# Output projection in two halves with reordered weight splits, and a down product in groups of up to four tile pairs, in a hybrid decoder layer

## The chip, the core and the metric

The kernel runs on one core of a Trainium2 chip. Its engines are TensorE (PE, with its weight loads shown as PEld), VectorE (DVE), ScalarE (ACT), GpSimd (POOL) and SyncE (SP), whose queue issues the DMAs. The metric is the device time of one execution in microseconds; the median of three runs before the change is 1321.57 us (1320.02 to 1322.45). The profile is one execution of its own, of 1318.76 us.

## The reference

One layer of a decoder step over 1088 tokens (1024 of a prompt, 8 x 8 of decoding), with model width 1024 and all values in fp32:

```python
hn = rms_norm(x, norm_mix_gain)
proj = hn @ w_in
...                                   # retention (8 heads) -> o_r, windowed attention (8 heads) -> o_s
h = x + jnp.concatenate([o_r, o_s], axis=-1) @ w_out
hf = rms_norm(h, norm_ffn_gain)
h = h + jnp.square(jax.nn.relu(hf @ w_up)) @ w_down      # 1024 -> 4096 -> 1024
```

The retention state and the key and value caches are outputs too. The change touches the output projection (`w_out`), the second norm and the two products behind it.

## The kernel before

**Precision.** Each fp32 operand of a matmul is split into a high part (an ACT cast, L754) and a low part (a subtraction, L755), and a product is three matmuls (`mm3`, L179 to L181): high by high, low by high, high by low. `halve` does a split, `wsplit` does it for a 128 x 512 piece of weights, and its last argument names the engine of the low part. Split weights lie in two rings of four buffers, `wa` and `wb`; the raw ones come through `rawload` into rings of three.

**Tokens.** They are worked on as two sets `s` of 544, each as two halves `h` of `Q` = 272. A tile `m` is 128 of the 1024 output features.

**Order.** The program is traced by Python, and a scheduler that simulates the engines puts each engine's instructions in order: program order is the priority, each engine and DMA queue then runs its list in order and waits on semaphores. Buffers of a pool that is closed are given to a later pool tile by tile, when their last user is done.

**Retention and first token set.** For blocks t = 5, 6, 7 a retention block runs, then `out_proj(0, m)` for two tiles, then `mix_block`, which stores the gated retention output (`mr_hi_d`, `mr_lo_d`). `mix_load(s, half, pool)` reads the mix of a token set back: half "a" is attention, "r" is retention. `out_proj` loads one tile of weights (`wo_raw`, 1024 columns), splits its two halves, and for each h adds up eight k-blocks, the attention half first, in one accumulator in PSUM. Then it adds the input (`y`), stores the result (`y_d`) for the end, multiplies by the norm's gain (`f`) and adds squares to `acc`.

**Second token set.** `operands(0, m)` for all m forms the seven right operands B11, B21, B22, T1 to T4 of the up product (a seven-product scheme over 2 x 2 blocks) from `f`, split by ACT and DVE (`op_0h`, `op_0l`). Then `mix_load(1, "r")` and, for each m, `out_proj(1, m)` and `operands(1, m)`. `norm(s)` sums `acc` over the partitions with small matmuls, takes the power −0.5 on POOL, writes the result to `r_d` in DRAM in two DMAs and reads it back, spread over all partitions, as `rsf` in a third. For the second set it stands inside the first `up`.

**Up product.** `up(fp)` for fp = 0 to 15: `left` loads the weights of one of 16 column blocks (`wu`), forms combinations on POOL (`comb`, L932) and gives seven split pieces in the order `PROD`. Each meets the operands of both token sets in accumulators `psx`, `psy`, `psz`. DVE, ACT and POOL form the squared ReLU and its combinations `rt`, stored to `u_d`.

**Down product.** Eight groups g of two row blocks of `w_down` (`wd0a`, `wd0b`, ...). For each of seven products, in the order `DOWN`, the piece of each row block is split (low part on POOL), `ur` is loaded from `u_d` and split into `uh` and `ul`, and 4 x 2 accumulators `psd` take six matmuls each. After each product each accumulator is added to one of four sums `a` by DVE (L1045), or copied there by ACT (L1043) the first time; the accumulators go on through several products. `yt` (the stored `y_d`) is added at the end of groups 1 to 6, two or three tiles each.

The lines that set the order at the two hand-overs before:

```python
for m in range(8):
    operands(0, m)
mx0x.close()
operand_tiles(1)
mix_load(1, "r", ox.enter_context(pool("mxR", side="right")))
for m in range(8):
    out_proj(1, m, late)
    operands(1, m)
    if m == 1:
        norm(0)
```

Of the kernel before, what the change touches and what calls it, by code (L numbers as in the profile page):

```python
# [2 lines left out]

# [32 lines left out]
def hymba_layer(ctx: ExitStack, tc: tile.TileContext, a: dict, o: dict):  # L36
# [725 lines left out]
    def rawload(src, name, tag="raw", pl=None):  # L762
        raw = (pl or mw).tile([P, 1024], F32, tag=tag, name=name, bufs=3)
        nc.sync.dma_start(raw, src)
        return raw
# [11 lines left out]
    def out_proj(s, m, psum):  # L777
        raw = rawload(a["w_out"][m], f"wo{s}_{m}_raw")
        w = [wsplit(raw[:, i * 512 : i * 512 + 512], "wa", f"wo{s}_{m}_{i}", nc.vector) for i in range(2)]
        y = om.tile([P, 2, Q], F32, tag="y", name=f"y{s}_{m}", bufs=2)  # L780
        nc.sync.dma_start(y.rearrange("p h n -> p (h n)"), a["xY"][:, s, m, :])
        for h in range(2):
            ps = psum()
            for k in (4, 5, 6, 7, 0, 1, 2, 3):
                lh, ll = (w[k // 4][:, i, k % 4 * 128 : k % 4 * 128 + 128] for i in range(2))
                mh, ml = (mix[s, ("r" if k < 4 else "a") + x][:, k % 4, h, :] for x in "hl")
                mm3(ps, lh, ll, mh, ml, k == 4, k == 3)
            nc.vector.tensor_tensor(y[:, h, :], ps, y[:, h, :], ALU.add)
# [14 lines left out]

    def operands(s, m):
# [11 lines left out]
        else:  # L816
            put(B21, f[:, 0, :])
            put(B22, f[:, 1, :])
            b12, t1 = fs[s, kk][:, 1, :], fs[s, kk][:, 0, :]
            nc.gpsimd.tensor_tensor(t1, f[:, 1, :], t1, ALU.subtract)  # L820
            put(T2, t1)
            nc.gpsimd.tensor_tensor(f[:, 0, :], f[:, 0, :], t1, ALU.subtract)
            put(T4, f[:, 0, :])
            nc.gpsimd.tensor_tensor(f[:, 1, :], f[:, 1, :], b12, ALU.subtract)
            put(T3, f[:, 1, :])

    def norm(s):

        ps = psM.tile([P, 512], F32, tag="b", name=f"psr{s}")
        accf = acc[s].rearrange("p h n -> p (h n)")  # L830
        for i, r in enumerate((0, 128, 256, 384, 416)):
            col_sums(ps[:, i : i + 1], accf[:, r : r + 128], ones[:, 0:1])
        rf = (rst, nsinks)[s][:, 0:5]
        nc.vector.tensor_scalar(rf, ps[:, :5], 1.0 / 1024.0, EPS, ALU.mult, ALU.add)
        rsqrt_inplace(rf, 5)
        c0 = 2 * Q * s
        nc.sync.dma_start(r_d[c0 : c0 + 512].rearrange("(t p) -> p t", p=128), rf[:, :4])
# [30 lines left out]
    mx0 = mx0x.enter_context(pool("mx0", side="right"))  # L868
    mix_load(0, "a", mx0)
    mix_load(1, "a", mxA)  # L870
    mix_block(4, *held[4])
    mix_load(0, "r", mx0)
    early = lambda: psA.tile([P, 512], F32, tag="mm", name="pso")[:, :Q]
    for t in (5, 6, 7):
        mt = retention_block(t)
        for m in (2 * t - 10, 2 * t - 9):
            out_proj(0, m, early)
        mix_block(t, *mt)
    mix_block(8, *mt8)
    for m in (6, 7):  # L880
        out_proj(0, m, early)
# [24 lines left out]
    late = lambda: bank("pso")  # L906
    operand_tiles(0)
    for m in range(8):
        operands(0, m)
    mx0x.close()  # L910
    operand_tiles(1)
    mix_load(1, "r", ox.enter_context(pool("mxR", side="right")))
    for m in range(8):
        out_proj(1, m, late)
        operands(1, m)
        if m == 1:
            norm(0)
    ox.close()


    mid = ctx.enter_context(pool("u", side="right"))

    def left(order, src, name, lo_eng, raw_tag="raw", raw_pool=None, s_tag="S", s_pool=None, tags=("wa", "wb")):
# [6 lines left out]
        def comb(i, p_, q_, op):  # L930
            t_ = have[i] = (s_pool or mid).tile([P, 512], F32, tag=s_tag, name=f"{name}_s{i}", bufs=4)
# [11 lines left out]

    def up(fp):
        gen = left(PROD, a["w_up"][fp], f"wu{fp}", nc.vector)
# [229 lines left out]
```

## Time and profile before

| what | value |
|---|---|
| median of three runs | 1321.57 us |
| the profiled execution | 1318.76 us, span of its instructions 1317.0 us |
| PE busy | 1227.8 us (93%) |
| DVE busy | 842.5 us (64%) |
| POOL busy | 696.0 us (53%) |
| ACT busy | 504.5 us (38%) |
| DMA | 178.96 MB, 136 GB/s in the mean |

Times in the views are counted from the start of the span. By the lines of the kernel, the early projection begins at about 434, the last projection matmul starts at 594.5, the up product ends at 951 and the down product runs to the end. In a row of groups, `out<-in` are the tiles by their names in the program with numbers left out, then partitions x elements, `x` the count, busy time, mean time of one in ns, and the engine's idle time before them with what ended it. A wait is put down to the releaser that came last. PEclk is the granted share of the full clock of TensorE.

### The profile page before, as it was taken

How to read it: one execution, taken by the hardware profiler on the slowest of the kernel's cores; microseconds unless marked ns; L12 is line 12 of the kernel's file. 1: busy time of each engine (PE TensorE's matmuls, PEld its weight loads, DVE VectorE, ACT ScalarE, POOL GpSimd, SP SyncE). 2: the span in 40 equal slices, each digit the busy share in tenths (PEclk: the TensorE clock that was granted, in tenths of full speed). 3: DMA queues.
4: the chain of work that ended last, by engine and by line, in shares of the span. 5: the costliest groups of instructions: out<-in, count | busy, mean ns of one | idle time of the engine just before them, and what ended most of it. 6: DMA issues, size and time to landing. Idle time of an engine off the chain costs nothing.

```text
span 1317.0 us, 24166 instructions
## 1 busy us (share of the span) xinstructions
PE 1227.8 (93%) x9581; PEld 1161.9 (88%) x9581; DVE 842.5 (64%) x1549; ACT 504.5 (38%) x1027; POOL 696.0 (53%) x542
## 2 busy tenths in 40 slices
PE   7989999999998698595999999999959999999998
PEld 5979877778978698595999999999959999999998
DVE  8736645543136567486666666767455888888886
ACT  5333334354213324153444344444444333333331
POOL 8325232222324423225566666656685887789761
PEclk9989999999999899698999999999989999999999
DMA  6211223324405855562243424243544445545434
GB/s 222 66 55 56 76 78 96 114 79 127 124 35 183 283 185 166 117 186 71 108 152 124 171 105 183 93 183 112 202 159 142 154 157 178 167 153 157 142 103 170
DMA packets 112778, 178.96 MB, mean 136 GB/s; under 512 B 14048, under 2 KB 82592, under 8 KB 112408
## 3 DMA queue, kind: packets, MB, share of 16 engines
q1 hardware_dynamic: 112663, 177.41, 41.1%
q8 instruction: 75, 1.23, 0.4%
q14 instruction: 40, 0.32, 0.1%
HBM read 119.31 MB, written 58.07 MB: 135 GB/s over the span
## 4 chain that ended last, share of the span: by engine, by line
PE 77%; DMA 8%; DVE 7%; POOL 5%; issue 1%; ACT 1%; SPq 0%; DVEq 0%; ACTq 0%; POOLq 0%
PE psd L181 7%; PE psd L179 7%; PE psd L180 7%; PE psx L179 5%; PE psx L181 5%; PE psx L180 5%; PE psf L181 3%; PE psf L179 3%; PE psf L180 3%; PE psz L181 2%; PE psz L179 2%; PE psz L180 2%; PE pst L179 2%; PE pst L180 2%; PE pst L181 2%; PE po L421 2%
## 5 line engine op out<-in xcount | busy, mean ns | idle before, releaser
L1045 DVE TENSOR_TENSOR a<-a,psd 128x272 f32<-128x272 f32 x416 | 162.4, 429 | 43.8 <-PE psd L181 43.3
L755 DVE TENSOR_TENSOR ul<-ur,uh 128x1088 fp32r<-128x1088 f32 (+1 forms) x57 | 108.5, 1908 | 25.9 <-ACT uh L754 23.7
L367 POOL TENSOR_TENSOR sp<-sp,ssp 128x1024 f32<-128x1024 f32 (+1 forms) x16 | 28.6, 1787 | 110.0 <-DVE ssp L366 110.0
L179 PE MATMUL psx<-op_1h,wu_w 128*128 128x272 f32 x256 | 75.0, 293 | 7.1 <-ACT m L974 7.1
L755 DVE TENSOR_TENSOR wu_w<-wu_s,wu_w 128x512 fp32r<-128x512 f32 x64 | 69.9, 1093 | 15.9 <-ACT wu_w L754 14.7
L179 PE MATMUL psx<-op_0h,wu_w 128*128 128x272 f32 x256 | 74.9, 292 | 0.0
L181 PE MATMUL psx<-op_1l,wu_w 128*128 128x272 f32 x256 | 74.7, 292 | 0.0
L181 PE MATMUL psx<-op_0l,wu_w 128*128 128x272 f32 x256 | 74.5, 291 | 0.0
L180 PE MATMUL psx<-op_1h,wu_w 128*128 128x272 f32 x256 | 74.3, 290 | 0.0
L180 PE MATMUL psx<-op_0h,wu_w 128*128 128x272 f32 x256 | 74.1, 289 | 0.0
L961 DVE SCALAR_TENSOR_TENSOR m<-m,rsf 128x272 f32<-128x272 f32 x96 | 61.8, 644 | 11.9 <-DMA rsf<-r_d 9.2
L754 ACT CAST uh<-ur 128x1088 fp32r<-128x1088 f32 (+1 forms) x57 | 61.8, 1087 | 9.0 <-PE psd L180 9.0
L181 PE MATMUL psf<-hnl,wqk_hi 128*128 128x384 f32 (+1 forms) x192 | 65.0, 339 | 0.0
L995 POOL TENSOR_TENSOR rt<-rt 128x272 f32<-128x272 f32 x64 | 64.3, 1014 | 1.2
L179 PE MATMUL psf<-hnh,wqk_hi 128*128 128x384 f32 (+1 forms) x192 | 64.9, 338 | 0.0
L180 PE MATMUL psf<-hnh,wqk_lo 128*128 128x384 f32 (+1 forms) x192 | 64.8, 338 | 0.0
L995 POOL TENSOR_TENSOR rt<-r,rt 128x272 f32<-128x272 f32 x32 | 31.7, 992 | 62.0 <-ACT r L962 62.0
L755 DVE TENSOR_TENSOR wu_w<-wu_r,wu_w 128x512 fp32r<-128x512 f32 x48 | 41.6, 868 | 27.5 <-ACT wu_w L754 27.5
L179 PEld LDWEIGHTS psx<-op_1h,wu_w 128*128 128x128 f32 x256 | 48.8, 191 | 7.3 <-ACT m L974 7.3
L956 DVE TENSOR_TENSOR m<-m,psz 128x272 f32<-128x272 f32 x64 | 28.0, 437 | 41.5 <-ACT m L974 26.6
L754 ACT CAST wu_w<-wu_s 128x512 fp32r<-128x512 f32 x64 | 39.8, 622 | 37.4 <-PE psy L181 30.5
L403 DVE SCALAR_TENSOR_TENSOR sp<-dtab,nsl,scp 128x256 f32<-128x256 f32 (+1 forms) x64 | 28.5, 459 | 37.4 <-PE scp L402 37.0
(511 smaller groups left out, 4902.8 us busy)
## 6 DMA issues: line engine op xcount, KB each, us to landing
u_d<-rt SPq DMA_DIRECT2D x32, 952.0 KB, 5.7
ur<-u_d SPq DMA_DIRECT2D x56, 544.0 KB, 4.0
wu_r<-in_w_up SPq DMA_DIRECT2D x32, 512.0 KB, 4.2
wo_raw<-in_w_out SPq DMA_DIRECT2D x16, 512.0 KB, 4.1
y<-in_xY SPq DMA_DIRECT2D x16, 272.0 KB, 3.0
y_d<-y SPq DMA_DIRECT2D x16, 272.0 KB, 2.4
yt<-y_d SPq DMA_DIRECT2D x16, 272.0 KB, 3.6
out_yT<-a SPq DMA_DIRECT2D x16, 272.0 KB, 2.2
```

The costliest lines, as they stand in the source:

```text
L179: nc.tensor.matmul(ps, lh, rh, start=first, stop=False, skip_group_check=more)
L180: nc.tensor.matmul(ps, ll, rh, start=False, stop=False, skip_group_check=more)
L181: nc.tensor.matmul(ps, lh, rl, start=False, stop=last, skip_group_check=more)
L367: nc.gpsimd.tensor_tensor(s, s, ss.unsqueeze(2).broadcast_to([P, 4, n]), ALU.mult)
L403: nc.vector.scalar_tensor_tensor(s[:, g, :], dtab[:, 256 - n :], nsl[:, c, kv, g : g + 1], pg, ALU.mult, ALU.add)
L421: nc.tensor.matmul(po[p_, :], vs[:, c - 1 + h, p_], pts[kv][:, h, :], start=h == halves[0], stop=h == 1)
L754: nc.scalar.copy(hi, src)
L755: lo_eng.tensor_tensor(lo, src, hi.bitcast(F32), ALU.subtract)
L956: nc.vector.tensor_tensor(t_, t_, bank_, ALU.add)
L961: nc.vector.scalar_tensor_tensor(t_, src, 0.0, rsf[:, s, h, :], ALU.max, ALU.mult)
L995: sub = lambda o_, p_, q_: nc.gpsimd.tensor_tensor(o_, p_, q_, ALU.subtract)
L1045: nc.vector.tensor_tensor(to, to, ps, ALU.add)
```

## The change

The projection's weights are loaded for two tiles at a time and one half of the rows at a time (`wo_pair`). For the first token set the splits of a tile pair are drawn one tile ahead (`out_early`), and the second set's attention mix is loaded after block 6 and not at the start. For the second set, the attention halves of tiles 0 to 3 are accumulated first, in eight open accumulators; then four of the eight operand tiles of set 0 are formed, the retention mix is loaded, and the rest follows in pairs of tiles, with the other four operand tiles between them. The first two pieces of up weights are split before the last two residuals. `norm` spreads its result by matmuls with a broadcast operand and copies, and not by way of DRAM. In `operands` B22 comes last.

The down product runs in five groups of 2, 4, 4, 4 and 2 row blocks: each accumulator takes up to twelve matmuls before it is added to the sums. The weights' low parts are formed by DVE. The ring `rawb` has nine buffers instead of three, `Sb` ten instead of four. The `yt` adds stand at the end of groups 1 and 2, eight each. The up stage's own tiles get a pool that is closed with it.

```diff
-    def out_proj(s, m, psum):
-        raw = rawload(a["w_out"][m], f"wo{s}_{m}_raw")
-        w = [wsplit(raw[:, i * 512 : i * 512 + 512], "wa", f"wo{s}_{m}_{i}", nc.vector) for i in range(2)]
+    def wo_pair(s, m, half):
+        raw = mw.tile([P, 1024], F32, tag="raw", name=f"wo{half}{s}_{m}_raw", bufs=3)
+        c0 = 512 * (half == "a")
+        nc.sync.dma_start(
+            raw.rearrange("p (m n) -> p m n", m=2), a["w_out"][m : m + 2, :, c0 : c0 + 512].rearrange("m p n -> p m n")
+        )
+        for i in range(2):
+            yield wsplit(raw[:, i * 512 : i * 512 + 512], "wa", f"wo{half}{s}_{m + i}", nc.vector)
+
+    def out_half(s, half, ps, h, w, first, last):
+        for k in range(4):
+            lh, ll = (w[:, i, k * 128 : k * 128 + 128] for i in range(2))
+            mh, ml = (mix[s, half + x][:, k, h, :] for x in "hl")
+            mm3(ps, lh, ll, mh, ml, first and k == 0, last and k == 3)
+
+    def residual(s, m, pss):
         y = om.tile([P, 2, Q], F32, tag="y", name=f"y{s}_{m}", bufs=2)
...
+    def out_parts(s, ms, half, psum, pss):
+        for m in ms:
+            if m % 2 == 0:
+                gen = wo_pair(s, m, half)
+            w = next(gen)
+            for h in range(2):
+                if half == "a":
+                    pss[m, h] = psum()
+                out_half(s, half, pss[m, h], h, w, half == "a", half == "r")
...
     def norm(s):
-        rsqrt_inplace(rf, 5)
-        c0 = 2 * Q * s
-        nc.sync.dma_start(r_d[c0 : c0 + 512].rearrange("(t p) -> p t", p=128), rf[:, :4])
-        nc.sync.dma_start(r_d[c0 + 512 : c0 + 544].rearrange("(p t) -> p t", t=1), rf[96:128, 4:5])
-        nc.sync.dma_start(
-            rsf[:, s, :, :].rearrange("p h n -> p (h n)"), r_d[c0 : c0 + 544].unsqueeze(0).broadcast_to([P, 544])
-        )
+        rsqrt_inplace(rf, 6)
+        for h in range(2):
+            pb = psM.tile([P, 512], F32, tag="b", name=f"psn{s}{h}")
+            for i, (c0, n) in enumerate(((0, 128), (128, 128), (256, 16))):
+                nc.tensor.matmul(
+                    pb[:, c0 : c0 + n], rf[:, 3 * h + i : 3 * h + i + 1].broadcast_to([P, 128]), ident[:, 128 - n :],
+                    start=True, stop=True,
+                )
+            nc.scalar.copy(rsf[:, s, h, :], pb[:, :Q])
...
+    def out_early(m):
+        if m % 2 == 0:
+            gens["a"], gens["r"] = (wo_pair(0, m, x) for x in "ar")
+            ahead.extend(next(gens[x]) for x in "ar")
+        wa_, wr_ = ahead
+        ahead.clear()
+        if m % 2 == 0:
+            ahead.extend(next(gens[x]) for x in "ar")
+        pss = [early() for h in range(2)]
+        for h in range(2):
+            out_half(0, "a", pss[h], h, wa_, True, False)
+            out_half(0, "r", pss[h], h, wr_, False, True)
+        residual(0, m, pss)
...
     mix_load(0, "a", mx0)
-    mix_load(1, "a", mxA)
...
+        if t == 6:
+            mix_load(1, "a", mxA)
         mix_block(t, *mt)
...
+    pss = {}
+    out_parts(1, range(4), "a", late, pss)
+    for m in (2, 6, 3, 7):
+        operands(0, m)
+    mx0x.close()
+    operand_tiles(1)
+    mix_load(1, "r", ox.enter_context(pool("mxR", side="right")))
+    rest = [0, 4, 1, 5]
+    for ms in ((0, 1), (2, 3), (4, 5), (6, 7)):
+        if ms[0] > 3:
+            out_parts(1, ms, "a", late, pss)
+        out_parts(1, ms, "r", late, pss)
+        if ms == (6, 7):
+            gen0 = left(PROD, a["w_up"][0], "wu0", nc.vector, tags=("wa", "wa", "wb", "wb"))
+            ready = [next(gen0), next(gen0)]
+        for m in ms:
+            residual(1, m, [pss[m, h] for h in range(2)])
+            if rest:
+                operands(0, rest.pop(0))
+            operands(1, m)
+        if ms == (2, 3):
+            norm(0)
...
-    for g in range(8):
-        gens = [
-            left(DOWN, a["w_down"][2 * g + 1], f"wd{g}b", nc.gpsimd, "rawb", dn, "Sb", dn, ("wb",)),
-            left(DOWN, a["w_down"][2 * g], f"wd{g}a", nc.gpsimd, tags=("wa",)),
-        ]
+    for g, (f0, nf) in enumerate(((0, 2), (2, 4), (6, 4), (10, 4), (14, 2))):
+        gens = []
+        for f in range(nf):
+            own = ("rawb", dn, "Sb", dn) if f else ("raw", mw, "S", mid)
+            gens.append(left(DOWN, a["w_down"][f0 + f], f"wd{f0 + f}", nc.vector, *own, tags=("wb" if f % 2 else "wa",)))
...
-                    for f in range(2):
+                    for f in range(nf):
...
-        for n in range(16):
-            if n * 6 // 16 + 1 == g:
+        if g in (1, 2):
+            for n in range(8 * g - 8, 8 * g):
```

More of the change, by code (lines that the diff above doesn't have):

```diff
@@ L2 @@
 from contextlib import ExitStack
+from itertools import chain
 import numpy as np
@@ L782, in out_proj @@
         for h in range(2):
[L783 to L788, printed above, removed]
+            nc.vector.tensor_tensor(y[:, h, :], pss[h], y[:, h, :], ALU.add)
         kk, k2 = m % 4, m // 4
@@ L942, in left @@
             yield wsplit(have[i], tags[n % len(tags)], f"{name}_w{i}", lo_eng)
+    late = lambda: bank("pso")
+    operand_tiles(0)
+    pss = {}
[20 more added lines that the diff above has]
+            norm(0)
+    ox.close()
+    mid = ctx.enter_context(pool("w", side="right"))
+    ux = ExitStack()
+    um = ux.enter_context(pool("u", side="right"))
     def up(fp):
[L945 removed]
+        gen = chain(ready, gen0) if fp == 0 else left(
+            PROD, a["w_up"][fp], f"wu{fp}", nc.vector, tags=("wa", "wa", "wb", "wb"))
         x, y, z = ([bank(f"ps{n}{s}") for s in range(2)] for n in "xyz")
         home = {1: (x, True), 2: (y, True), 6: (x, False), 5: (z, True), 7: (x, False), 4: (x, False), 3: (z, False)}
[L948 removed]
+        rt = [um.tile([P, 7, Q], F32, tag="rt", name=f"rt{fp}_{s}", bufs=2) for s in range(2)]
         held, wait = {}, []
         def tq(n, s):
[L952 removed]
+            return um.tile([P, Q], F32, tag="tq", name=f"{n}{fp}_{s}", bufs=10)
         def add(n, s, bank_):
@@ L1004, in hymba_layer @@
     opx.close()
+    ux.close()
     dn = ctx.enter_context(pool("dn", side="left"))
```

64 lines of the change are left out of this document (23 added, 41 removed).

## The prediction

> **What bounds the kernel now.** I read the page first, for the share of each engine.
>
> ```profile
> span 1317.0 us, 24166 instructions
> PE 1227.8 (93%) x9581; PEld 1161.9 (88%) x9581; DVE 842.5 (64%) x1549; ACT 504.5 (38%) x1027; POOL 696.0 (53%) x542
> ```
>
> The matrix engine PE is busy for 93%, but an average over stages hides where it stops. So the second view is the table of windows, one row for each stage that the change touches: columns are busy us and instructions of PE, weight loads, DVE, ACT, POOL, then granted clock, DMA share and GB/s.
>
> ```profile
> 415.00:507.00 92.00, 76.72 (x748) 71.87 (x747) 59.71 (x135) 28.22 (x48) 30.23 (x22) 0.91 0.72 234
> 507.00:595.00 88.00, 67.53 (x520) 66.60 (x519) 58.46 (x106) 34.19 (x78) 30.66 (x32) 0.84 0.57 152
> 595.00:629.00 34.00, 19.97 (x164) 19.30 (x163) 21.23 (x29) 12.41 (x29) 18.58 (x15) 0.77 0.26 63
> 629.00:951.00 322.00, 322.00 (x2551) 321.81 (x2551) 207.09 (x316) 139.17 (x316) 202.93 (x182) 1.00 0.38 142
> 951.00:992.00 41.00, 23.51 (x157) 22.63 (x157) 20.62 (x8) 17.50 (x40) 32.78 (x28) 0.83 0.54 186
> 992.00:1317.00 325.00, 318.56 (x2549) 317.90 (x2547) 262.59 (x484) 112.63 (x162) 232.01 (x149) 1.00 0.48 151
> ```
>
> From 629 to 951 (the up product) PE never stops: 322/2551 = 0.126 us per matmul. At that pace the other stages need: 507–595, 520 x 0.126 = 65.5 of 88 us (22.5 lost); 595–629, 20.7 of 34 (13.3 lost); 951–992, 19.8 of 41 (21.2 lost); 992–1317, 321.2 of 325 (3.8 lost). In 415–507, where small matmuls of the retention are mixed in, PE is idle for 92 − 76.7 = 15.3 us. So about 76 us can be had at all, nearly all of it in the three hand-overs: retention to output projection, projection to up, up to down. The clock falls to 0.77–0.84 there, so the loss is more than the idle time. The waits of PE name the places (total us, times, longest):
>
> ```profile
> PE pso L179 <- DMA mixrh<-mr_hi_d: 11.9, 2, 10.3
> PE psd L181 <- DVE ul L755: 11.3, 1, 11.3
> PE pso L180 <- DVE wo L755: 10.7, 3, 6.1
> PE psx L179 <- ACT m L974: 7.1, 1, 7.1
> PE psy L179 <- ACT wu_w L754: 4.3, 1, 4.3
> PE pso L179 <- ACT wo L754: 3.9, 2, 3.7
> PE psd L179 <- DVE a L1045: 2.6, 2, 1.6
> PE psy L180 <- DVE wu_w L755: 2.6, 1, 2.6
> ```
>
> **The change, part by part.** Matmuls of the projection and the down product, weight loads and bytes stay the same in number; what moves is order, owner and latency.
>
> *A, start of the projection (415–507).* Loading the second token half's attention mix moves from the head of the queue to behind block 6.
>
> ```profile
> 420.00:430.00 10.00, 6.90 (x76) 6.10 (x76) 7.65 (x19) 2.37 (x4) 4.50 (x4) 0.83 1.06 396
> 417.84 0.62 SPq L773
> 418.51 0.85 SPq L773
> 419.41 14.14 DMA wo_raw<-in_w_out
> ```
>
> The first two rows of the chain are the issues of this pair (128 x 4 x 544 fp32 each, 2.2 MB); the first projection weights queue behind them and land 14.14 us later, with the DMA engines full at 396 GB/s. 2.2 MB at 396 GB/s is 5.6 us. The first `wo` splits, and the q/k loads of the next retention block behind them, come 5.6 us sooner; PE's 3.7 us wait for `wo` goes, and the retention chain is late next. The pair lands later, at a DMA share below this one. Each early pair of tiles now needs two raw loads, but each holds two tiles' halves: the same 512 KB per tile. Bounds: −2 (the moved pair delays block 7's loads) to +12; I take a gain of 5.
>
> *B, projection of the second token half and its operands (507–604).*
>
> ```profile
> 507.00:604.00 97.00, 71.29 (x582) 69.91 (x580) 66.66 (x118) 40.34 (x93) 36.58 (x38) 0.85 0.52 141
> L755 DVE TENSOR_TENSOR op_1l<-f,op_1h 128x272 fp32r<-128x272 f32 x28 | 17.2, 649 | 1.5 <-ACT op_1h L754 1.5
> L755 DVE TENSOR_TENSOR op_0l<-f,op_0h 128x272 fp32r<-128x272 f32 x28 | 17.0, 657 | 1.2 <-DMA y<-in_xY 1.2
> 537.36 0.33 SPq L764 DMA_DIRECT2D wo_raw<-in_w_out  x1
> 538.38 0.38 SPq L837 DMA_DIRECT2D r_d<-rst  x1
> 538.86 13.68 DMA mixrh<-mr_hi_d
> ```
>
> Before, all 28 splits `op_0l` stand ahead of the next weights on DVE, so PE waits for `wo` (10.7 in all); then `mixrh` is issued at 538.86, behind a weight load and the norm's `r_d` on SP, lands 13.68 us later, and PE waits 10.3. After, four tiles' attention halves run first: 4 x 2 x 12 matmuls = 96 x 0.126 = 12.1 us of PE work that needs neither, and it covers both waits. `norm(0)` and its DMAs come behind the load. The other half of the operands is dealt out between the later tiles. What is late next is DVE: its work is the same 66.7 us, and without gaps it would end at 507 + 66.7 = 573.7 instead of 604. Eight accumulators stay open until DVE's residual adds close them, so PE will wait for DVE at times. I take DVE filled to 81% (as the down product fills it: 262.6/325), 82 us, so the operands end at 589: a gain of 15. Bounds: 0 (same gaps) to 30 (none).
>
> *C, into the up product (595–629).* The chain there:
>
> ```profile
> 607.47 1.56 POOL nsinks L133
> 609.47 9.47 DMA r_d<-nsinks
> 618.99 4.84 DMA rsf<-r_d
> L626 PE MATMUL pkr<-c_ident,kt 128*128 128x128 f32 x24 | 4.3, 299 | 0.0
> L974 ACT COPY m<-psx 128x272 f32<-128x272 f32 x94 | 35.4, 382 | 39.6 <-PE psx L181 39.5
> ```
>
> The norm's way through DRAM takes from 609.03 to 623.83, 14.8 us; it becomes six matmuls (nearest row, a transpose of one block, 0.299) and two copies of 0.382: 1.8 + 0.8, with hand-overs about 3 us. It is 12 us shorter, and three issues leave SP. New is that PE's queue holds matmuls that wait for POOL's 1.56 us power, with the up product behind them: 0 to 4 us for each norm, by the order. Two up weights are split before the last residual, so the `wu_w` waits (4.3 + 2.6) go. `B22` is put last, and is needed last. The stage's loss is 13.3, of which 10 go; bounds 2 to 13.3.
>
> *D, into the down product (951–992).*
>
> ```profile
> 971.32 15.34 DVE L755 TENSOR_TENSOR ul<-ur,uh 128x1088 fp32r<-128x1088 f32 x2 [11.81 <-ACT uh L754]
> L755 DVE TENSOR_TENSOR ul<-ur,uh x57: 812/1566/14142, 955.7 to 1302.3; 128x1088 fp32r<-128x1088 f32 x55, 128x544 fp32r<-128x544 f32 x2
> 972.00 1.29 POOL L932 TENSOR_TENSOR wd1a_s<-wd1a_s,wd1a_r 128x512 f32<-128x512 f32 x1
> ...
> 983.06 1.25 POOL L932 TENSOR_TENSOR wd1b_s<-wd1b_r,wd1b_r 128x512 f32<-128x512 f32 x1
> u_d<-rt SPq DMA_DIRECT2D x32, 952.0 KB, 5.7
> ```
>
> One `ul` takes 14.14 us where the median is 1.57: POOL runs without a gap beside it, its last instruction in the row ends at 984.3, and `ul` ends at 985.5. PE waits 11.3 of it. The weights' low parts leave POOL, so its ready queue shrinks: of the ten in this row, four are splits (their `w` tiles). But POOL keeps the 16 `rt` subtractions and now may work ahead on ten `Sb` tiles: up to 10 x 1.27 = 13 us in a row, so a shorter stall can come back. Also the new pool (nine raw, ten `Sb` buffers) is larger than the operands' space and reaches into that of the up stage, so an accumulator may wait for the last `u_d` store, whose landing takes 5.7 us: 0 to 5.7. Bounds −4 to +18; I take 12.
>
> *E, inside the down product (992–1317).*
>
> ```profile
> L1045 DVE TENSOR_TENSOR a<-a,psd 128x272 f32<-128x272 f32 x416 | 162.4, 429 | 43.8 <-PE psd L181 43.3
> L755 DVE TENSOR_TENSOR ul<-ur,uh 128x1088 fp32r<-128x1088 f32 (+1 forms) x57 | 108.5, 1908 | 25.9 <-ACT uh L754 23.7
> L1053 DVE TENSOR_TENSOR a<-a,yt 128x544 f32<-128x544 f32 x16 | 17.3, 1084 | 8.2 <-DMA yt<-y_d 8.0
> L755 DVE TENSOR_TENSOR wu_w<-wu_s,wu_w x58: 679/1180/1267, 629.8 to 934.3; 128x512 fp32r<-128x512 f32 x58
> ```
>
> Five groups instead of eight: 5 x 56 evictions, 32 of them copies, so 248 DVE adds instead of 416 (−168 x 0.429 = −72 us). Against it 112 splits come from POOL. Cheapest: 112 x 0.679 = 76; dearest, 112 x 1.267 = 142 (the up stage's largest). POOL was busy 63% in the up stage (202.9/322) and has only 64 combinations left here, 64 x 1.27 = 81 us, 24% of the stage; scaling the excess with POOL's share gives about 0.85 a split (95 us), and `ul` falls from its mean of 1.9 to about 1.5 (56 x 1.5 = 84). DVE: 248 x 0.429 + 95 + 84 + 17 = 302 us, beside PE's (157 + 2549) x 0.126 = 341. PE stays the bound; the split's price is hidden by it. The eight `yt` adds in a row in two groups can hold DVE for a load each, but a four-pair group gives DVE 7 x 12 x 0.126 = 10.6 us before a bank is needed again. Gain 0; bounds +3.8 and the rival below.
>
> **The sum.** 5 + 15 + 10 + 12 + 0 = 42. The profiled execution took 1318.76 us (span 1317.0): 1276.8. The median shown, 1321.57, is 2.8 higher, so I forecast 1280.
>
> **Rivals.**
> 1. *Slower: DVE becomes the bound of the down product.* It decides if a split's mean goes over (341 − 106 − 84 − 17)/112 = 1.2 us, near the dearest row (1.267), or less if DVE, in order, keeps its 44 us of waiting for PE: then 302 + 44 = 346 already touches 341. At the dear end, 349 + 44 = 393, 52 over 341; against gains of 30 elsewhere that is 1321.6 + 52 − 30 = 1344; half of it gives 1318. For it: DVE was 81% busy here (262.6/325). Against: POOL, which makes splits dear, loses most of its work. 0.12.
> 2. *The projection's gain is eaten by DVE's queue.* Both kinds of operands and the residual adds compete, PE stalls on open accumulators; B gives 0–3 and C 5: 1321.6 − 5 − 2 − 5 − 12 = 1298. For it: DVE is 69% busy there (66.7/97). 0.18.
> 3. *The port stall returns at the start of down* with the new work-ahead: D is 0, 1292. 0.17.
> 4. *More than forecast*: A to D come to their upper bounds, 12 + 30 + 13.3 + 18 = 73, 1248. For it: PE alone would need no more. Against: DVE's order would have to be without gaps. 0.07.
> 5. *The stall at the start of down goes wholly.* If DVE gets its port after one POOL instruction (1.3 us), the long `ul` came from something that does not return, and D gains 18: 1274. Against: the long `ul` itself, which outlasted ten POOL instructions. 0.08. The Trainium skill states such a rule, "SBUF — State Buffer", section "SBUF: two separate sides": DVE with two SBUF inputs and GpSimd take a shared port pair as a lock for one whole instruction, and the other blocks. By that rule the sum would be 1274, by the trace's 14.14 us it is 1280, and the measurement decides. The same rule speaks against the change in E, since it turns 112 splits into instructions of the kind that block and are blocked; the rows above price that.
> The forecast itself, 1265–1290, has 0.38.
>
> **How the numbers follow.** Leaving out the dear half of rival 1 and the far end of rival 4, the range is 1254–1314. A change of 0.2% (2.6 us) is about what can be told. Slower needs rival 1 near its dear end: 0.08; within 0.2%: its middle, 0.04; faster: 0.88.
>
> **What would show it.** A: the first `wo_raw` lands in under 10 us and PE's `wo` wait goes. B: no PE wait for `mixrh` over 2 us, operands done before 590 less A's gain. C: no `r_d` DMA of the norm; under 4 us between the power and the `rsf` copies; PE at full clock within 10 us of the last projection matmul. D: no `ul` over 4 us, first 40 us of down at over 280 matmuls. E: DVE near 300 us, POOL near 100, PE waits on L1045's successor below 4. Wrong if PE in the down product waits on DVE for more than 10 us, or if a new single wait over 10 us stands in a hand-over.

## The result, and the profile after

The changed kernel takes 1312.86 us in the median of five runs (1309.19 to 1316.79), the kernel before 1322.14 beside it (1320.02 to 1323.84): ratio 0.9935, 95% interval 0.9907 to 0.9963. That is 9.3 us faster where 42 were forecast. The profiled execution took 1311.57 us. Its page and its windows, with the columns of before:

```profile
span 1309.3 us, 24034 instructions
PE 1233.3 (94%) x9621; PEld 1167.0 (89%) x9621; DVE 832.6 (64%) x1492; ACT 496.5 (38%) x1030; POOL 529.6 (40%) x430
```

```profile
415.00:507.00 92.00, 79.23 (x756) 73.89 (x756) 60.25 (x136) 28.82 (x49) 31.52 (x23) 0.91 0.71 230
507.00:595.00 88.00, 70.30 (x564) 69.65 (x563) 61.82 (x110) 36.76 (x85) 31.61 (x33) 0.88 0.47 155
595.00:629.00 34.00, 28.43 (x245) 27.81 (x244) 25.87 (x37) 15.48 (x36) 23.51 (x19) 0.85 0.19 63
938.00:990.00 52.00, 32.44 (x228) 31.72 (x229) 28.77 (x27) 25.02 (x54) 35.41 (x26) 0.80 0.67 233
990.00:1309.00 319.00, 315.87 (x2511) 315.65 (x2509) 251.12 (x413) 106.23 (x152) 65.36 (x42) 1.00 0.44 143
```

In 507 to 595 PE is busy only 2.8 us more than before; from 595 to 629 it gains 8.5. In 938 to 990, the way into the down product, 19.6 us are still empty. The waits of PE name why:

```profile
PE psd L180 <- ACT uh L755: 19.4, 2, 17.2
PE pso L180 <- DMA mixrh<-mr_hi_d: 13.2, 1, 13.2
PE rsr L180 <- ACT qkb L608: 9.1, 5, 3.3
PE psn L860 <- POOL rst L134: 2.9, 1, 2.9
```

Two single waits of over 10 us stand in the hand-overs again: the one for `mixrh` is longer than before (10.3), and one of 17.2 us for `uh` has taken the place of the 11.3 for `ul`. The queue of SP shows both places, first at the mix, then at the end of the up product:

```profile
535.17 0.34 SPq L796 DMA_DIRECT2D y<-in_xY  x1
537.77 0.37 SPq L782 DMA_DIRECT2D wor_raw<-in_w_out  x1
538.19 0.57 SPq L774 DMA_DIRECT2D mixrh<-mr_hi_d  x1
...
944.41 0.33 SPq L765 DMA_DIRECT2D wd_r<-in_w_down  x1
946.67 4.42 SPq L1056 DMA_DIRECT2D u_d<-rt  x2
951.14 1.38 SPq L765 DMA_DIRECT2D wd_r<-in_w_down  x2
952.62 0.83 SPq L1080 DMA_DIRECT2D ur<-u_d  x1
```

`mixrh` goes out at 538.19 (before 538.86), and `ur` at 952.62, behind the last two stores `u_d`. Marks from the traces (start of a matmul, us), for the kernels that the text needs:

| kernel | last projection matmul | matmul 130 of up | last of up | first of down | matmul 200 of down | end |
|---|---|---|---|---|---|---|
| before | 594.5 | 630.3 | 952.7 | 955.7 | 999.3 | 1317.0 |
| changed | 590.9 | 618.5 | 944.2 | 961.7 | 992.6 | 1309.3 |
| norm_alone | 587.6 | 615.1 | 938.0 | 941.0 | 985.4 | 1302.5 |
| f67_in_rsf | 580.8 | 608.4 | 933.5 | 950.8 | 982.3 | 1299.0 |
| two_pools | 591.7 | 619.3 | 948.3 | 952.2 | 989.7 | 1306.4 |
| old_down | 587.9 | 617.1 | 939.5 | 943.0 | 973.4 | 1292.0 |
| proj_f67_dve_all | 577.5 | 607.0 | 935.0 | 938.4 | 968.4 | 1286.2 |

### The profile page after: what moved, and what is told of

Same layout as the page of the kernel before. It is cut to its first block, busy times and chain, and to the rows that moved or that the text cites. A ratio compares the mean times of both kernels' runs of the same rounds, so it can differ in the third digit from the quotient of the medians.

```text
span 1309.3 us, 24034 instructions
## 1 busy us (share of the span) xinstructions
PE 1233.3 (94%) x9621; PEld 1167.0 (89%) x9621; DVE 832.6 (64%) x1492; ACT 496.5 (38%) x1030; POOL 529.6 (40%) x430
## 4 chain that ended last, share of the span: by engine, by line
PE 67%; DMA 10%; DVE 8%; POOL 7%; issue 4%; ACT 3%; SPq 0%; ACTq 0%; POOLq 0%; DVEq 0%
PE psd L181 9%; PE psd L180 9%; PE psd L182 9%; POOL rt L1051 6%; DMA u_d<-rt 6%; PE psf L182 3%; PE psf L180 3%; PE psf L181 3%; PE pst L180 2%; PE pst L181 2%; PE pst L182 2%; PE po L422 2%; PE psx L181 2%; PE psx L182 2%; PE psx L180 2%
## 5 line engine op out<-in xcount | busy, mean ns | idle before, releaser
L180 PE MATMUL psd<-uh,wd_w 128*128 128x272 f32 x896 | 259.8, 290 | 19.4 <-ACT uh L755 19.4
L181 PE MATMUL psd<-uh,wd_w 128*128 128x272 f32 x896 | 260.8, 291 | 0.0
L182 PE MATMUL psd<-ul,wd_w 128*128 128x272 f32 x896 | 256.0, 289 | 0.0
L180 PEld LDWEIGHTS psd<-uh,wd_w 128*128 128x128 f32 x896 | 170.9, 191 | 19.8 <-ACT uh L755 19.8
L181 PEld LDWEIGHTS psd<-uh,wd_w 128*128 128x128 f32 x896 | 170.3, 190 | 0.0
L182 PEld LDWEIGHTS psd<-ul,wd_w 128*128 128x128 f32 x896 | 168.1, 189 | 0.3 <-DVE ul L756 0.3
L1099 DVE TENSOR_TENSOR a<-a,psd 128x272 f32<-128x272 f32 x248 | 102.4, 432 | 47.4 <-PE psd L182 47.4
L756 DVE TENSOR_TENSOR wu_w<-wu_s,wu_w 128x512 fp32r<-128x512 f32 x64 | 62.6, 981 | 95.9 <-ACT wu_w L755 95.8
L756 DVE TENSOR_TENSOR ul<-ur,uh 128x1088 fp32r<-128x1088 f32 x56 | 86.9, 1580 | 2.9 <-ACT uh L755 2.9
L755 ACT CAST wd_w<-wd_s 128x512 fp32r<-128x512 f32 x64 | 37.3, 618 | 111.1 <-PE psd L182 77.6
L1018 ACT ACTIVATE rt<-m 128x272 f32<-128x272 f32 x64 | 26.0, 427 | 111.1 <-DMA u_d<-rt 104.1
L956 POOL TENSOR_TENSOR wd_s<-wd_r,wd_s 128x512 f32<-128x512 f32 x16 | 24.6, 1538 | 104.5 <-DVE wd_w L756 103.3
```

The source lines that it names most:

```text
L180: nc.tensor.matmul(ps, lh, rh, start=first, stop=False, skip_group_check=more)
L181: nc.tensor.matmul(ps, ll, rh, start=False, stop=False, skip_group_check=more)
L182: nc.tensor.matmul(ps, lh, rl, start=False, stop=last, skip_group_check=more)
L755: nc.scalar.copy(hi, src)
L756: lo_eng.tensor_tensor(lo, src, hi.bitcast(F32), ALU.subtract)
L956: nc.gpsimd.tensor_tensor(t_, p_, q_, op)
```

## The experiments

All ratios are to the kernel before, run beside each, with their 95% intervals; that kernel's medians lay between 1320.4 and 1321.4.

### What holds the load of the retention mix back

`f67_low` only moves the addresses of `f6` and `f7`, so that the new mix covers exactly the old one:

```diff
+    f67 = {m: mx0.tile([P, 2, Q], F32, tag=f"f{m}", name=f"f0_{m}") for m in (6, 7)}
     mix_load(0, "a", mx0)
...
-            f = mx0.tile([P, 2, Q], F32, tag=f"f{m}", name=f"f{s}_{m}")
+            f = f67[m]
```

> The change as it is, with one thing different: the two scaled tiles f6 and f7 of the first token set lie below the mix tiles in their pool, so that the second set's retention mix no longer overlaps them. Queue theory: the load of that mix stays where it is in SP's list, behind the input tile y_1 and the weights wor_4, because the list holds it back until the last reader of the whole closed pool is placed. It is issued at 538 us (within 1), PE waits 13 us for it, the time stays within 2 us of the changed kernel's (0.992 to 0.995 of the kernel before). Address theory: the overlap was what it waited for; it is issued at 519 to 525, PE's wait falls below 4 and the time falls by 8 to 10 us (ratio 0.985 to 0.988).

Measured: 1313.56 us, 0.9948 (0.9929 to 0.9967); the load stays where it was, and PE's wait is 13.5 us.

```profile
538.56 0.57 SPq L774 DMA_DIRECT2D mixrh<-mr_hi_d  x1
```

`f67_in_rsf` takes both tiles out of the pool:

```diff
-            f = mx0.tile([P, 2, Q], F32, tag=f"f{m}", name=f"f{s}_{m}")
+            f = rsf[:, m - 6]
```

> The change, with f6 and f7 of the first token set in the still unused norm tile (rsf) and not in the pool of the first set's mix. Queue theory: that pool's last reader is now PE's last retention matmul of the first set at 518, so the load of the second set's retention mix stands ahead of y_0, woa_4 and wor_4 in SP's list, is issued at 515 to 521 (538 before), lands by 532, and PE's single wait of 13.2 us falls below 4. The last projection matmul starts 7 to 11 us sooner (591 to about 582) and the time falls by 6 to 10 us (ratio to the kernel before 0.986 to 0.989). Rival, DVE paces the stage: the load is sooner but DVE's operands and weight splits end where they did; another wait of PE (for a weight split or a bank) takes the place, the last projection matmul stays within 3 us of 591, the time within 3 us.

Measured: 1299.98 us, 0.9848 (0.9826 to 0.9869). Its SP queue and its window:

```profile
517.96 0.57 SPq L774 DMA_DIRECT2D mixrh<-mr_hi_d  x1
```

```profile
507.00:595.00 88.00, 75.39 (x638) 74.41 (x638) 68.60 (x121) 40.18 (x93) 38.91 (x39) 0.91 0.50 157
```

The load goes out 20 us sooner, the wait for it is gone, and 638 matmuls run in the window instead of 564. Since the address alone changes nothing, it is the place in SP's list: here and in the next pair of runs, a load into the space of a closed pool stands behind the last readers of that pool, here the splits of `f6` and `f7`, and so behind `y`, `woa` and `wor` loads that wait for DVE. The section on the kernel before says that a closed pool's buffers are given on tile by tile; for the place in the queue's list it is the whole pool that counts. The same edit with the old projection and the norm by matmuls:

> The kernel before with two of the edits: the norm by matmuls, and f6 and f7 of the first set in the norm tile; the projection's old order stays. Theory: in the old order, too, the closed pool's last reader holds the retention mix back in SP's list; the load is issued at 515 to 522 (538.9 before), PE's wait of 10.3 us goes, the last projection matmul comes 5 to 11 us sooner than with the norm alone (587.6), and the time is 1292 to 1299 (ratio 0.978 to 0.983). Rival: in the old order all 28 operand splits stand ahead of the weights on DVE, PE waits for those instead (the 10.7 us for wo become 15 or more), and the gain is below 3 us.

Measured: 1304.53 us, 0.9890 (0.9875 to 0.9905), no better than the norm alone (below). `mixrh` goes out at 520.51, but norm_alone leaves PE only 1.0 us of waiting for this mix (for `mixrl`), so there was next to nothing to save, and the wait for the first norm's power grows from 5.2 us to 7.5:

```profile
PE psn L839 <- POOL rst L133: 7.5, 1, 7.5
```

The rival's time came (a gain below 3 us), its reason did not: PE waits 11.6 us for `wo` splits here and 10.4 in norm_alone. So the early load is worth 11.5 us by the ratios in the change's order, and nothing in the old order with this norm.

### What holds the u loads back

`ur_low` swaps addresses, `two_pools` lets the first tiles of down depend on the operands' pool alone:

```diff
-            ws = [next(gen) for gen in gens]
             ur = dn.tile([P, 4, 2, Q], F32, tag="ur", name=f"ur{g}_{i}", bufs=2)
+            ws = [next(gen) for gen in gens]
```

> The change, with the space of ur put below that of the nine raw weight tiles in the down product's pool, over operands of the first token set that are read earlier in the last up step. Queue theory: the two ur loads stay behind the last two u_d stores in SP's list, are issued at 952 to 954, and the first matmul of the down product stays at 960 to 963, the time within 2 us of the changed kernel's. Address theory: ur waited for its space; it is issued before 947, PE's wait of 17.2 us for uh shrinks to below 10, the first matmul of down comes 6 to 10 us sooner and the time falls by as much (ratio 0.986 to 0.989).

Measured: 1312.1 us, 0.9933 (0.9912 to 0.9953); the loads stay behind the stores.

```profile
953.97 1.76 SPq L1080 DMA_DIRECT2D ur<-u_d  x2
```

`two_pools`:

```diff
     opx.close()
-    ux.close()
     dn = ctx.enter_context(pool("dn", side="left"))
+    ux.close()
+    dn2 = ctx.enter_context(pool("dn2", side="left"))     # Sb, a, yt
```

> The change, with the down product's pool in two: raw weights, ur, uh and ul in a first one that needs only the operands' space, combinations, sums and yt in a second one that is opened when the up stage's tiles are given up. Queue theory: the weights wd1 and the two ur loads now stand ahead of the last two u_d stores in SP's list; ur is issued at 943 to 948 (952.6 before), the first matmul of down starts at 952 to 956 (961.7) and the time falls by 5 to 9 us (ratio 0.986 to 0.990). Rival, the space: ur lies over operands that are read late in the last up step, so that it is issued no sooner than 950 and the gain is below 3 us. Second rival: the 14 us stall of ul returns, because DVE then forms ul while POOL works on combinations without a gap; the first matmul moves but matmuls 24 to 200 of down lose it again.

Measured: 1304.21 us, 0.9869 (0.9848 to 0.9891).

```profile
942.60 3.24 SPq L1081 DMA_DIRECT2D ur<-u_d  x2
950.75 0.33 SPq L1056 DMA_DIRECT2D u_d<-rt  x1
```

`ur` goes out ahead of the stores, the first matmul of down starts at 952.2 instead of 961.7. The queue theory holds, by the same mechanism as at the mix. No long `ul` came.

### The attention mix, and three edits together

`mix_tied` makes the second set's attention mix wait for block 6:

```diff
+            if behind is not None:
+                nc.vector.tensor_copy(t_[:, 0, 0, 0:1], behind[:, 0:1])
...
-            mix_load(1, "a", mxA)
+            mix_load(1, "a", mxA, mt[0])
```

> The change, with the load of the second set's attention mix really held until block 6: DVE first writes one column of its tiles from a result of block 6. Theory A: in the changed kernel this pair still goes out at 421 and 432 us and makes the next retention block's q load take 13.5 us; held back, that load takes under 9 us, the first projection matmul comes 3 to 6 us sooner (431 to 425 to 428) and the end of the first set's projection 3 to 6 us sooner (517.7), the time falls by 3 to 6 us against the changed kernel (ratio to the kernel before 0.989 to 0.991). Rival: the retention chain of small matmuls, DVE and POOL paces the stage; the first matmul moves, but the end of the first set's projection stays within 2 us of 517.7 and the time within 2 us.

Measured: 1312.38 us, 0.9933 (0.9921 to 0.9945): nothing. The `q` load lands after 11.59 instead of 13.47 us, PE's wait for `qkb` in 415 to 520 falls from 8.8 to 3.5, but a wait of 3.1 for the first set's own retention mix takes over, and the last projection matmul of the first set starts at 518.0 (517.7). The rival holds for the time and for this mark; the first projection matmul, which was to move in both, did not (431.1, 431.3 before the edit).

> The change with three edits together: f6 and f7 in the norm tile, the down product's pool in two, the second attention mix held until block 6. If the places are independent, the ratios add: 0.9848 + 0.9869 - 0.994 = 0.978 (1292 us) from the first two, and 0.974 to 0.978 with the third (1286 to 1292). If they share a bound (DVE in the hand-overs, the DMA engines), it comes out above 0.981 (1296).

Measured: 1295.5 us, 0.9811 (0.9796 to 0.9825), at the boundary that was set for a shared bound: about 4 us of the gains are lost.

### The parts alone

> The kernel before with one part of the change: the norm spread by matmuls and not by way of DRAM. Theory: this part is the larger share of the change's gain; the last projection matmul stays at 594 (within 2 us), matmul 130 of the up product comes 8 to 12 us sooner (630 to about 620), the time falls by 7 to 11 us (ratio 0.992 to 0.995). Rival: the gain at the start of up came from the weights split ahead and B22 put last, and the norm alone gives less than 4 us (ratio above 0.997).

The edit is the function `norm` of the change in the kernel before. Measured: 1304.29 us, 0.9871 (0.9857 to 0.9886): 17 us where 7 to 11 were expected, more than the whole change gives. By the marks, 6.9 us come already before the last projection matmul, which was expected to stay. The DMA view of 530 to 580, first of before, then of this kernel (KB each, median us to landing):

```profile
DMA packets 4258, 7.41 MB, mean 148 GB/s; under 512 B 844, under 2 KB 1896, under 8 KB 4255
mixrh<-mr_hi_d SPq DMA_DIRECT2D x1, 1088.0 KB, 13.7
r_d<-rst SPq DMA_DIRECT2D x1, 2.0 KB, 8.1
r_d<-rst SPq DMA_DIRECT2D x1, 0.1 KB, 15.3
```

```profile
DMA packets 4378, 8.75 MB, mean 175 GB/s; under 512 B 304, under 2 KB 1814, under 8 KB 4374
mixrh<-mr_hi_d SPq DMA_DIRECT2D x1, 1088.0 KB, 7.6
```

The first set's norm sends 540 more packets under 512 bytes, most of them by the 2 KB store that is issued just ahead of the mix (538.38 and 538.86 in the prediction's rows). In the trace of before, packets of the mix's load behind them take up to 8.5 us each, where 0.09 is usual. Without them the same 1088 KB land in 7.6 us instead of 13.7, and PE's 10.3 us wait goes, partly replaced by 5.2 us for the norm's power. In projection_alone, which keeps these stores but issues them behind the mix, it lands in 8.4.

> The change's projection part alone: projection by halves, operands interleaved, B22 last, two up weights split ahead; the norm by way of DRAM and the down product are those of the kernel before. Theory: the part is worth nothing, because the load of the second set's retention mix stays where it was; the last projection matmul starts within 3 us of 594 and the time stays within 0.3% of the kernel before (ratio 0.997 to 1.003). Rival: it is worth the 8 us and more that two weights split ahead and a cover of 12 us of matmuls should bring (ratio below 0.994).

Measured: 1324.35 us, 1.0003 (0.9973 to 1.0033). Of twelve executions, five lie at 1312.4 to 1314.4 and seven at 1322.9 to 1329.0; the profiled one took 1326.57 and has one `ul` of 14.12 us. So the part is worth nothing in the median, as expected; that the five faster executions lack the stall is inferred, since none of them was profiled. One mark missed: the last projection matmul starts at 586.7, 7.8 us sooner than before. It brings nothing, because the second norm's way through DRAM ends only 1.5 us sooner (the load of `rsf` is issued at 617.44, before at 618.99), and matmul 130 of up starts at 629.5 (630.3).

> The change with the old down product (eight groups of two, low parts on POOL, three raw buffers). Theory: the new down product is worth nothing as it stands, since its shorter start is lost again to the ur loads behind the stores; the time stays within 4 us of the changed kernel's (ratio 0.991 to 0.997), a single ul of 10 to 15 us is back beside POOL work, and there are about 520 evictions. Rival: the new down product does bring the forecast 12 us, and something else in the change costs as much; then this kernel is 8 to 14 us slower than the changed one (ratio above 0.999).

Measured: 1308.31 us, 0.9874 (0.9831 to 0.9917), again in two groups: 1293.8 and 1293.9, and 1307.3 to 1311.7. Neither expectation came: with the old down product the change is 8 us faster by the ratios, though the intervals touch, and the profiled execution, 1293.8, has no long `ul`. Here is the same place in norm_alone, with the stall (DVE, then first and last of POOL's ten beside it), and in old_down without:

```profile
956.62 15.33 DVE L755 TENSOR_TENSOR ul<-ur,uh 128x1088 fp32r<-128x1088 f32 x2 [11.86 <-ACT uh L754]
957.27 1.29 POOL L934 TENSOR_TENSOR wd1a_s<-wd1a_s,wd1a_r 128x512 f32<-128x512 f32 x1
...
968.33 1.26 POOL L934 TENSOR_TENSOR wd1b_s<-wd1b_r,wd1b_r 128x512 f32<-128x512 f32 x1
```

```profile
958.18 1.84 DVE L756 TENSOR_TENSOR ul<-ur,uh 128x1088 fp32r<-128x1088 f32 x1 [11.11 <-PE psd L182]
957.59 1.28 POOL L756 TENSOR_TENSOR wd0b_w<-wd0b_r,wd0b_w 128x512 fp32r<-128x512 f32 x1
958.84 2.33 POOL L956 TENSOR_TENSOR wd1a_s<-wd1a_s,wd1a_r 128x512 f32<-128x512 f32 x1
```

In the second, DVE gets its turn after POOL's instruction ends at 958.87, and POOL's next one takes 2.33 instead of 1.29 us; in the first, POOL goes on in steps of 1.25 us, and the first `ul` of the row, 14.12 of its 15.33 us, ends at 970.74, after POOL's run (969.59). In all four profiles with a long `ul` (before, norm_alone, projection_alone, norm_f67) it ends 1.1 to 1.2 us after the last instruction of POOL's run. POOL has much the same work there in both kernels. The two groups of times suggest that whether DVE gets a turn differs from execution to execution; of the six only one was profiled, so this is not shown.

### The owner of the low parts, and the size of the groups

```diff
-            left(..., f"wd{g}b", nc.gpsimd, "rawb", dn, "Sb", dn, ("wb",)),
+            left(..., f"wd{g}b", nc.gpsimd if g else nc.vector, "rawb", dn, "Sb", dn, ("wb",)),
```

(and the same for `wd{g}a`), on top of norm_alone:

> The kernel before with the norm by matmuls, and with the low parts of the down product's first group formed by DVE and not by POOL; all later groups stay on POOL. Theory: a ul of DVE gets no turn while POOL has work without a gap; with 14 fewer instructions in POOL's run at the start of down there is a gap, the single ul of 14.1 us is gone, matmul 200 of down comes 8 to 14 us sooner than with the norm alone (985.4), and the time falls from 1304.3 to 1290 to 1296 (ratio 0.976 to 0.981). Rival: POOL's ready combinations of the first two groups alone suffice, the long ul stays (10 us or more) and the time stays within 4 us of 1304.

Measured: 1292.75 us, 0.9802 (0.9785 to 0.9818); no `ul` over 2.4 us, matmul 200 of down at 970.4 (985.4). POOL has 14 instructions fewer in its run, and 9 us come by the ratios. With `f67` as well:

> The three small edits together on the kernel before: norm by matmuls, f6 and f7 in the norm tile, low parts of the first down group on DVE. If the two theories hold, the gains add: 1321 - 17 - 8 - 11 = 1285, within 1278 to 1292 (ratio 0.967 to 0.978), faster than the change as made by 20 us or more. If the long ul stays, 1292 to 1299.

Measured: 1297.2 us, 0.9824 (0.9811 to 0.9837). The gains do not add (1278 to 1292 was expected), though no `ul` is over 2.4 us: the early load with the old projection loses 3 to 4 us here, at the edge of the intervals; why was not found.

> The change with one thing undone: in the down product the weights' low parts go back to POOL (112 splits), the groups of four stay. Lock theory: POOL again has ten and more instructions in a row at the start of down or of the first group of four, and a single ul of 10 us or more is back; the time rises by 8 to 16 us over the changed kernel (1321 to 1329), in some runs perhaps not. Rival: the order of the groups and the later ur took the stall away, no ul over 5 us shows, and the time stays within 4 us of 1313. In the steady part DVE loses about 100 us of work and PE's pace of 0.125 a matmul stays, by both.

One word of the change undone (`nc.vector` to `nc.gpsimd`). Measured: 1307.5 us, 0.9911 (0.9882 to 0.9941), not slower than the change, no long `ul`. With the u loads in time:

> The change with the down pool in two (u loads in time) and the low parts of the down product back on POOL. Lock theory: ul now falls into POOL's run of combinations and splits, a ul of 10 us or more is back in at least some of the runs, whose times then lie 10 to 16 us above the others (about 1302 and 1315). Rival: the owner does not matter in groups of this order; no run stands out, no ul is over 5 us, and the time is 1298 to 1306.

Measured: 1304.61 us, 0.9871 (0.9852 to 0.9890), the four runs within 1301.6 to 1307.2, no long `ul`. Both times the rival holds. Here the third `ul` starts at 964.35, in a gap of POOL; in change_pool_low POOL has no gap and `ul` gets its turns all the same. In the new order no run here shows that the owner matters.

> The kernel before with the norm by matmuls and all low parts of the down product on DVE, in the old eight groups with their 416 sums. If splits on DVE cost about 1 us each (as in the changed kernel), DVE has 416 x 0.43 + 112 x 0.98 + 84 + 17 = 390 us of work in a stage that PE needs 340 us for: DVE becomes the bound, PE waits on the sums (L1047), and the time rises by 20 to 50 us over 1293. If they cost 0.69, because POOL no longer runs beside them, DVE has 358 us: 5 to 20 us more than 1293. Rival: DVE keeps below PE (330 or less, cheap ul and sums without POOL beside them) and the time stays within 4 us of 1293; then the larger groups bought nothing.

All low parts on DVE, eight groups. Measured: 1290.56 us, 0.9781 (0.9753 to 0.9808); the rival's time came. The steady part (990 to 1285), first the changed kernel, then this one:

```profile
990.00:1285.00 295.00, 295.00 (x2347) 295.00 (x2346) 236.09 (x381) 104.01 (x150) 65.36 (x42) 1.00 0.43 137
```

```profile
990.00:1285.00 295.00, 292.34 (x2325) 291.24 (x2324) 283.67 (x544) 99.60 (x139) 76.41 (x48) 1.00 0.49 152
```

DVE is busy 96% and PE loses at most 2.7 of 295 us. The old groups carry the splits; groups of four spare DVE 48 us in this stretch that nobody waits for.

> The change with f6 and f7 in the norm tile and the down pool in two (as before), and six raw buffers in the ring instead of nine. Theory: eight raw loads of the next group (4.2 MB) stand ahead of the third ur load in SP's list, so that matmuls 48 to 100 of down take 14 to 15 us where the old down product takes 6.6; with six buffers only four of them do, the third ur goes out before the two last of them and before yt, the stretch takes 7 to 11 us, and the time is 1288 to 1293 (ratio 0.974 to 0.979). Rival: the pieces of weights or the copies on ACT pace that stretch; it stays at 14 and the time at 1294 to 1298.

Measured: 1296.57 us, 0.9816 (0.9784 to 0.9849); matmuls 48 to 100 of down take 16.8 us (14.9 in all_three, 6.6 in norm_dve0). The raw loads are not the reason. `uh` is cast at 956.85 instead of 959.57, but PE then waits 5.8 us for weights that ACT casts behind it. The order of casts and copies on ACT is one candidate; it was not tried.

The two candidates, projection and norm of the change, `f67_in_rsf`, and the old down product with low parts on DVE for the first group, or for all:

> The change's projection and norm, with f6 and f7 in the norm tile; the down product is the old one, with the low parts of its first group on DVE. If the gains add: the last projection matmul at 578 to 582 (587.9 with the old projection), no long ul, down as with norm_dve0; 1292.75 less 6 to 9 is 1284 to 1287 (ratio 0.971 to 0.975), the fastest of all. Rival: the earlier end of the projection is lost again in the up product or at the start of down (as f67 lost 4 us with the old projection), 1290 to 1297.

> The change's projection and norm, f6 and f7 in the norm tile, the old eight groups of the down product with all low parts on DVE. If the places are independent: 1287.5 less the 2 us that all splits on DVE gave with the old projection, 1283 to 1288 (ratio 0.971 to 0.976), PE waiting less than 5 us in all on DVE's sums. Rival: DVE at 96% holds PE when the start of down is tighter; 1290 or more.

Measured: 1287.47 us, 0.9770 (0.9739 to 0.9802), and 1287.95 us, 0.9749 (0.9729 to 0.9769). They cannot be told apart, and beat both the kernel before (by 33 us) and the change (by 22 to 25, by the ratios). The second ends the projection at 577.5, and PE waits 0.4 us for DVE's sums.

## Why the prediction was right or wrong

**Where the 42 us went.** By the marks of the two profiles the change gains 3.6 us up to the last projection matmul, where A and B were to give 20, and 8.2 from there to matmul 130 of up (C: 10). It loses 3.3 in the rest of up, for which the sum had no term, and 1.8 from there to matmul 200 of down, where D was to gain 12; behind that 1.0 comes (E: 0). The steps that failed are B's cover of a load that the change left at its place in SP's list, with 13.2 us of waiting, and D's price of 0 to 5.7 us for the larger pool, which cost 17.2. That the time still lies at the edge of the stated range is no merit of the working.

**A (5) came to nothing, though both its marks came.** The first weights land in 8.6 us, PE's 3.7 us for `wo` are gone, and the first projection matmul starts at 431.3 instead of 434.8. What failed is that the q load comes 5.6 us sooner too. "Moves from the head of the queue to behind block 6" is true of the program and not of the queue: the pair went out behind the first weights, at 421.24 and 431.67, since nothing kept it longer, and the q load landed at 436.2 (437.1 before). The last projection matmul of the first set starts only 0.6 us sooner (517.7). And where the pair was really held (mix_tied), the next wait took the gain.

**B (15) failed at one step**: that four tiles' attention halves "cover both waits". The cover ran, from 517.8 to 531.9; what it should cover moved nowhere and landed at 545.0, since the load kept its place behind DVE's splits, all 28 of which again came first (515.5 to 538.4). "What is late next is DVE" skipped the load. The size was not far off: with the load free, operands end at 590.5 (589 forecast; 600.6 in the change) and 11.5 us come by the ratios.

**C (10) was right in kind and too small.** As forecast there is no `r_d` load, and 2.9 us lie between the power's end (602.78) and the last copy's start (605.65). But alone it gave 17: the term counted only the second norm's latency, which norm_alone bears out (8.3 us between the last projection matmul and matmul 130 of up), and left out what the first norm's small packets do to the mix load beside them. One mark fell: the granted clock is 0.82 from 591 to 605, 0.74 from there to 615 and 1.00 behind, so that full speed comes 24 us after the last projection matmul, and not 10.

**D (12) failed.** The long `ul` went, but in its place came 17.2 us for `uh`. The prediction saw that the new pool "reaches into that of the up stage", but charged it to an accumulator and at 0 to 5.7 us; in fact the weights and u loads of the whole pool were listed behind the last stores. The first 40 us of down hold about 273 matmuls (over 280 asked). The reason given for the stall's end, the owner, is not needed for it here (change_pool_low has none either), though in the old order the owner ends it (norm_dve0).

**E (0) was right**: PE is never held by the sums, and DVE has 280 us in 938 to 1309 where 302 were reckoned. But rival 1's condition was wrong: it kept 44 us of DVE's waiting for PE as if fixed; in norm_dve_all DVE is busy 96%, its sums wait 10.9 us for PE, and PE loses at most 2.7 of 295 us.

**The sum by parts.** The norm gives 14.5 us in the profiles. Against norm_alone, the change loses 3.3 us by the last projection matmul, 2.9 more by the end of up, 1.0 more by matmul 200 of down. The first of these is no chance of one execution: the mark lies at 587.9 to 593.0 in the seven profiles with this projection and this order of loads. The loss in up goes with ACT's waits for the `u_d` stores before it may write `rt` again (104.1 us in all, 29.7 in norm_alone). That was not tested, and proj_f67_dve_all speaks against it: with 76.7 us of such waits it takes still longer from matmul 130 of up to the last (328.0 us; 325.7 in the change, 322.9 in norm_alone).

**Rivals.** Rival 2 (1298) was right that B would give next to nothing, but named open accumulators and DVE's queue; PE waited for a load that SP's list held behind loads that wait for DVE. Rival 3's stall did not return in the change. Rival 5 and the rule of the Trainium skill ("SBUF — State Buffer", section "SBUF: two separate sides"), a lock for one whole instruction: the turns in old_down agree with it, the 14.12 us through ten POOL instructions in norm_alone do not. The rule does not say who is served next.

## What to carry to other kernels

Where a scheduler writes the queues, read the changed order before pricing a wait as covered: moving a line of the program moves nothing unless a dependency does, and with this scheduler a load into a closed pool's space inherits the latest reader of the whole pool. Look for the one tile whose life is longer than that of its neighbours, and give it another home: in the new order one line gave some 12 us. And measure the parts alone: the smallest part was worth more than the sum.

## What the runs showed of the hardware

Stores of 4-byte elements cost more than their own latency: with 540 packets under 512 bytes, 2 KB in all and most of them issued ahead, a 1088 KB load landed in 13.7 us and not in 7.6 (8.4 in projection_alone, which issues them behind it).

An `ul` of DVE took 12 to 14 us beside a row of POOL instructions without a gap in four profiles, and ended 1.1 to 1.2 us after the row. The times suggest that the same kernel runs with or without this stall: two of six executions of old_down lie 13 to 18 us below the other four, and one of 11 runs of the kernel before in one session at 1308.9 against 1317.9 to 1322.5, but of these only one of the two fast ones of old_down was profiled. With fourteen instructions fewer in POOL's row (norm_dve0) the profiled execution has no `ul` over 2.4 us, and all five runs lie at 1289.9 to 1296.4.
